# Gathering the experts of 32 more tokens, four experts of a token per gather, with dense products over 352 tokens

## The chip, the cores and the metric

The kernel runs on one core of one Trainium2 chip. The metric is device time in microseconds, from one launch, as the median of several runs. A separate profiled execution gives the trace; its own time stands beside its span below.

## The reference

One decoder layer over 512 tokens of width 1024: a combined input projection, differential attention and retention, an output projection, then PEER (product-key single-neuron experts), then a gated per-layer input and a last RMSNorm. The change touches PEER alone, which is:

```python
def peer(m, w_query, sub_keys, u, v):        # u, v: (16384, 1024) f32
    qry = (m @ w_query).reshape(B, S, PEER_HEADS, 2, PEER_KEY_DIM)
    scores = jnp.einsum('bshcd,hckd->bshck', qry, sub_keys)
    vals, idx = lax.top_k(scores, PEER_TOPK)            # 16 of 128 keys, twice
    ...
    top_s, top_pos = lax.top_k(cand, PEER_TOPK)         # 16 of 256 pairs
    expert = jnp.take_along_axis(cand_idx, top_pos, axis=-1)
    gates = jax.nn.softmax(top_s, axis=-1)
    ...
        act = jax.nn.gelu(jnp.einsum('cd,ced->ce', xt, u[e])) * g
        return jnp.einsum('ce,ced->cd', act, v[e])
```

Each token so has 8 heads x 16 = 128 experts out of 16384, each a row of `u` and a row of `v`. With `m` the normed input, the layer goes on as `h += peer(m)`, `h += sigmoid(rmsnorm(h) @ Wg + bg) * (p @ Wp)` and `out = rmsnorm(h)`.

## The kernel before

All is one function, `block_kernel`, with helpers inside. Four blocks of 128 tokens go through attention and the output projection; up to 368 us this has nothing to do with the change, but for `mtok` (line 920), the normed tokens of block 3.

PEER is computed in two ways. Blocks 0 to 2 (`NT = 3`, `ND = 384` tokens) go the dense way: for each of the 128 groups of 128 experts a product of U with all 384 tokens, Gelu, a multiplication by a map of gate weights (zero for experts that a token did not choose), and a product with V that is summed in PSUM. Block 3 goes the sparse way: each of its 128 experts per token is fetched by an indirect DMA of 128 rows, one row per token (`gather`, line 848), 4 KB each. A sparse step (`sparse_step`, line 853) is one VectorE instruction over 128x1024 elements: for `peer_u` a multiply and sum into a column of `act` (line 859), for `peer_v` a multiply and add into `yacc` (line 861). 256 of these steps are in the list `order` (lines 825 to 831), 128 of each kind.

Float32 products go over TensorE as three products of a high and a low part. For a U group (`products`, line 766, through `project` and `product3`, line 85) these are 24 matmuls with 128x128 of U as weights and 384 token columns moving; for a V group (line 782) 18 matmuls with 128 tokens of the activations as weights, 512 columns of V moving. `prepare` (line 736) makes the parts: ACT copies the high part `wh` (line 746), VectorE subtracts for the low part `wl` (line 762); for V groups VectorE also multiplies map and activation (`av`, line 752) and makes `al` (line 764), ACT makes `ah` (line 755). Weights are loaded by SP's queue four groups ahead (`RAW = 4`), their parts are made two ahead.

The first PEER stage (the loop at line 1190, 96 groups before) computes U groups only. Beside them `choose(b)` (line 1006) finds the 16 experts of each head, for block 3 first, and `weights_map(b, z)` (line 1111) builds the map, eight tokens in a pass: four VectorE instructions of 128x1024 (lines 1163 to 1166), 16 small matmuls (lines 1123, 1125), ACT copies to `gs` and `kept`. A map of 32 tokens is written to DRAM (`g_d`); activations of U groups past the first 24 are spilled to DRAM (`a_d`). What VectorE does between two groups is set by a small clock in the loop, which counts costs written in the code (`clock["pe"] += 4.1` for a group and so on). The number of groups in this stage comes out of that loop (`n_early`).

The second stage (the loop at line 1378) does the rest of the U groups and all V groups in the order of the list `seq`. Before it a budget is made: each load, write and gather of 512 KB counts `LOAD = 1.46`, `level` is the sum over the groups, and a sparse step is issued behind a group as long as

```python
            while done[0] < n_sp and (traffic + LOAD <= level * passed or n >= total - SPARSE_END):
                sparse_step()
                gather()
                traffic += LOAD
```

holds, so that the DMA traffic is spread evenly. Rows land in three buffers (`ROWS`), and in six more (`MORE`) from the time when the map's buffers are free until eight groups before `END = total - 64`; then the space goes to the closing part and three are left. Eight groups before the end the sparse sum is added to block 3 (`add_experts`, line 1258). Then follow the gate product, the sigmoid and the last norm (`turn`, `gate`, `close`).

Of the kernel before, what the change touches and what calls it, by code (L numbers as in the profile page):

```python
# [35 lines left out]
P = 128  # L36
S = 512
# [3 lines left out]
ND = NT * P  # L41
# [13 lines left out]
def block_kernel(ctx: ExitStack, tc, t):  # L55
# [89 lines left out]
    with pool("wa", 2, side="right") as wa, pool("sm", 2, side="right") as sm, \  # L145
# [553 lines left out]
        act = late.tile([P, P], F32, name="act")  # L699
        junk = late.tile([P, D], BF16, name="junk")  # L700
# [35 lines left out]
        def prepare(u, low):  # L736
            kind, i = u
            w = raw.pop(u)
            if kind == "g":
                for d in range(2):  # L740
                    c = slice(d * S, (d + 1) * S)
                    scaled_split(fin["gh"][i][d], fin["gl"][:, i, c], w[:, c], gains[:, G_PLE, i:i + 1])
                return
            wh = wt.tile([P, D], F32R, name="wh", tag="wh")
            wl = wt.tile([P, D], F32R, name="wl", tag="wl")
            nc.scalar.activation(wh, w, AF.Copy)  # L746
            parts[u] = wh, wl
            if kind == "v":
                gv, av = inputs.pop(u)
                if gv is not None:  # L750
                    av3 = av.rearrange("p (z t) -> p z t", t=RUN)
                    nc.vector.tensor_tensor(av3, gv, av3, op=OP.mult)  # L752
                ah = vp[0].tile([P, ND], F32R, name="ah", tag="ah", bufs=2)
                al = vp[0].tile([P, ND], F32R, name="al", tag="al", bufs=2)
                nc.scalar.activation(ah, av, AF.Copy)  # L755
                parts[u] += ah, al
            if low is nc.gpsimd:

                nc.scalar.activation(wl, w, AF.Copy, scale=-1.0)
                nc.gpsimd.dma_start(wl.bitcast(F32), w, accum_op=OP.add)  # L760
            else:
                low.tensor_tensor(wl, w, wh.bitcast(F32), op=OP.subtract)  # L762
            if kind == "v":
                nc.vector.tensor_tensor(al, av, ah.bitcast(F32), op=OP.subtract)  # L764
# [55 lines left out]
        vp, acc, count, done_u = [], [], [0], []  # L820
# [5 lines left out]
        for h in range(HEADS + 1):  # L826
            for k in range(TOPK):
                if h < HEADS:
                    order.append(("peer_u", h * TOPK + k))
                if h > 0:  # L830
                    order.append(("peer_v", (h - 1) * TOPK + k))
# [4 lines left out]
        def gather():  # L836

            while due:
                more = due.pop(0)
                if issued[0] >= n_sp or (more and not extra):  # L840
                    continue
                n = issued[0]
                issued[0] += 1
                table, r = order[n]
# [3 lines left out]
                nc.gpsimd.indirect_dma_start(out=rows[n], out_offset=None, in_=t[table],  # L848
                                             in_offset=bass.IndirectOffsetOnAxis(ap=e_sp[:, r:r + 1], axis=0))
# [3 lines left out]
        def sparse_step():  # L853
            n = done[0]
            done[0] += 1
            table, r = order[n]
            row = rows.pop(n)
            if table == "peer_u":
                nc.vector.tensor_tensor_reduce(junk, row, mtok, 1.0, 0.0, OP.mult, OP.add, act[:, r:r + 1])  # L859
            else:  # L860
                nc.vector.scalar_tensor_tensor(yacc, row, act[:, r:r + 1], yacc, op0=OP.mult, op1=OP.add)  # L861
            due.append(at_more.pop(n))
            if table == "peer_u" and r % TOPK == TOPK - 1:
                hs = slice(r + 1 - TOPK, r + 1)
                nc.scalar.activation(act[:, hs], act[:, hs], AF.Gelu)
                nc.vector.tensor_tensor(act[:, hs], act[:, hs], g_sp[:, hs], op=OP.mult)

        with pool("wp", 2, side="right") as wpp:
# [51 lines left out]
            nc.vector.tensor_tensor(mtok, mn[3], gffn, op=OP.mult)  # L920
    k_stack = ctx.enter_context(ExitStack())
    g_stack = ctx.enter_context(ExitStack())
    with pool("pk") as pk, pool("psG", 2, space=PSUM) as psG, pool("psT", space=PSUM) as psT:
# [74 lines left out]
        mh = pk.tile([P, ND], F16, name="mh")  # L998
        ml = pk.tile([P, ND], F16, name="ml")
        it = pk.tile([P, ND], BF16, name="it")  # L1000
        jt = pk.tile([P, ND], BF16, name="jt")
# [4 lines left out]
        def choose(b):  # L1006
# [77 lines left out]
            if b >= NT:  # L1084
# [4 lines left out]
                return  # L1089
            turned = []  # L1090
# [88 lines left out]
        def side():  # L1179
            yield from choose(3)  # L1180
            for b in range(NT):
                yield from choose(b)
                for z in range(P // RUN):
# [56 lines left out]
    def open_fin():  # L1240
# [10 lines left out]
        for name in ("gate_b", "final_gain"):  # L1251
            fin[name] = fp.tile([P, D], F32, name=name, bufs=1)
# [67 lines left out]
    with pool("acc", space=PSUM) as pa:  # L1320
        vp.append(mp)
        acc += [[pa.tile([P, S], F32, name=f"acc{b}{d}") for d in range(2)] for b in range(NT)]
# [30 lines left out]
        ends = [("hs", b) for b in (3, 0, 1, 2)] + [("final_gain", None), ("gate_b", None)]  # L1353
# [24 lines left out]
        for n, u in enumerate(seq):  # L1378
# [32 lines left out]
            if 0 <= n - end_at < len(ends):  # L1411
                name, b = ends[n - end_at]
                if b is None:
                    nc.sync.dma_start(fin[name], row_src(name))
                else:
                    nc.sync.dma_start(fin[name][:, b], sources[name][:, b])
# [96 lines left out]
```

## Time and profile before

| | us |
|---|---|
| median of 3 runs (lowest to highest) | 1546.71 (1545.36 to 1548.38) |
| the profiled execution: its time | 1544.91 |
| its span, first to last instruction | 1543.1 |
| TensorE busy | 1515.5 |
| VectorE busy | 1223.0 |
| ScalarE (ACT) busy | 676.4 |
| GpSimd (POOL) busy | 384.1 |
| DMA: bytes moved, mean over the span | 401.67 MB, 260 GB/s |
| granted TensorE clock, mean | 0.995 |

Busy time of TensorE is the union of its matmuls, whose ends are modelled: a matmul is drawn longer than the distance to the next. So the distance from start to start, or a piece of the chain divided by its matmuls, tells what one costs. The same holds in a small way for VectorE, where neighbours overlap by 0.08 us. The DMA share is the busy time of the 16 DMA engines over the stretch; packets overlap a little, so that it can read up to 1.03. A line number such as L85 can be that of a helper.

### The profile page before, as it was taken

What the parts mean: (1) busy time and instruction counts of PE and PEld (TensorE: products, weight loads), DVE (VectorE), ACT (ScalarE), POOL (GpSimd) and SP (SyncE); (2) the same over time, 40 slices, a digit from 0 to 9 for tenths busy, and PEclk for the clock granted to TensorE, in tenths of its full rate; (3) what the DMA queues carried; (4) which work ended last, traced back from release to release, by engine and by line L of the source; (5) the groups of instructions that cost most, each with busy time, mean ns of one, the idle gap of its engine ahead of it and who ended that gap; (6) DMA issues with size and microseconds to landing.
All of it is one profiled execution on the core that took longest, in us unless ns stands there. A gap on an engine that the chain in (4) does not pass through costs nothing.

```text
span 1543.1 us, 22928 instructions
## 1 busy us (share of the span) xinstructions
PE 1515.5 (98%) x8197; PEld 1342.0 (87%) x8197; DVE 1223.0 (79%) x2529; ACT 676.4 (44%) x1075; POOL 384.1 (25%) x321
## 2 busy tenths in 40 slices
PE   8999999999999999999999999999999999999996
PEld 6787887888999999999999989898988888888885
DVE  3767555779998999898985888988888885987755
ACT  4554645444634454453434333333333333453444
POOL 1300000110023203202224555554434311422000
PEclk9999999999999999999999999999999999999999
DMA  6412335773468979887999989999999988999601
GB/s 230 148 62 80 103 107 205 215 189 110 161 205 276 299 239 306 303 287 251 308 312 372 382 315 377 343 377 393 365 355 368 348 323 314 352 377 354 243 17 41
DMA packets 163378, 401.67 MB, mean 260 GB/s; under 512 B 14687, under 2 KB 77418, under 8 KB 163136
## 3 DMA queue, kind: packets, MB, share of 16 engines
q1 hardware_dynamic: 123248, 256.06, 46.7%
q0 software_dynamic: 40016, 144.15, 27.6%
q8 instruction: 64, 1.05, 0.3%
q14 instruction: 50, 0.41, 0.1%
HBM read 350.61 MB, written 42.21 MB: 255 GB/s over the span
## 4 chain that ended last, share of the span: by engine, by line
PE 88%; DVE 7%; DMA 3%; ACT 1%; issue 1%; SPq 0%; ACTq 0%; DVEq 0%
PE ps L85 44%; PE acc L782 31%; PE S L85 2%; PE S L322 2%; PE ps L518 1%; PE pg L1123 1%; PE pg L1125 1%; PE wo L85 1%; DVE wl L762 1%; PE sc L957 1%; DMA wraw<-in_w_val_dram 1%; DMA av<-a 1%; PE po L458 1%; PE po L639 1%; DMA wraw<-in_gate_w_dram 1%
## 5 line engine op out<-in xcount | busy, mean ns | idle before, releaser
L85 PE MATMUL ps<-xh,wh 128*128 128x384 f32 (+1 forms) x1312 | 464.0, 354 | 1.6 <-ACT av L810 0.8
L85 PE MATMUL ps<-xh,wl 128*128 128x384 f32 (+1 forms) x1312 | 457.3, 349 | 3.4 <-DVE wl L762 3.4
L85 PE MATMUL ps<-xl,wh 128*128 128x384 f32 (+1 forms) x1320 | 457.9, 347 | 0.0
L762 DVE TENSOR_TENSOR wl<-wraw,wh 128x1024 fp32r<-128x1024 f32 x260 | 317.4, 1221 | 77.5 <-ACT wh L746 76.8
L746 ACT ACTIVATE wh<-wraw 128x1024 fp32r<-128x1024 f32 x272 | 286.7, 1054 | 201.2 <-PE ps L85 94.7
L848 POOL DMA_INDIRECT row<-in_peer_u_dram,e_sp x128 | 174.0, 1359 | 360.6 <-DVE yacc L861 225.4
L848 POOL DMA_INDIRECT row<-in_peer_v_dram,e_sp x128 | 169.6, 1325 | 374.2 <-DVE act L859 277.3
L85 PEld LDWEIGHTS ps<-xh,wl 128*128 128x128 f32 x1312 | 247.4, 189 | 15.7 <-DVE wl L762 4.1
L85 PEld LDWEIGHTS ps<-xh,wh 128*128 128x128 f32 x1312 | 247.9, 189 | 13.9 <-ACT av L810 1.1
L85 PEld LDWEIGHTS ps<-xl,wh 128*128 128x128 f32 x1320 | 249.2, 189 | 10.2
L782 PE MATMUL acc<-wh,ah 128*128 128x512 f32 x768 | 237.1, 390 | 0.6 <-ACT ah L755 0.6
L782 PE MATMUL acc<-wl,ah 128*128 128x512 f32 x768 | 236.8, 390 | 0.0
L782 PE MATMUL acc<-wh,al 128*128 128x512 f32 x768 | 236.7, 390 | 0.0
L782 PEld LDWEIGHTS acc<-wl,ah 128*128 128x128 f32 x768 | 144.2, 188 | 30.1
L782 PEld LDWEIGHTS acc<-wh,al 128*128 128x128 f32 x768 | 144.2, 188 | 30.0 <-DVE al L764 0.2
L782 PEld LDWEIGHTS acc<-wh,ah 128*128 128x128 f32 x768 | 144.0, 188 | 30.1 <-ACT ah L755 1.0
L861 DVE SCALAR_TENSOR_TENSOR yacc<-row,act,yacc 128x1024 f32<-128x1024 f32 x128 | 163.9, 1280 | 2.0 <-DMA row<-in_peer_v_dram,e_sp 1.8
L859 DVE CUSTOM_DVE_ANT_0 junk<-row,mtok 128x1024 bf16<-128x1024 f32 x128 | 156.0, 1219 | 1.9 <-DMA row<-in_peer_u_dram,e_sp 1.6
L755 ACT ACTIVATE ah<-av 128x384 fp32r<-128x384 f32 x104 | 54.6, 525 | 228.5 <-PE acc L782 179.3
L764 DVE TENSOR_TENSOR al<-av,ah 128x384 fp32r<-128x384 f32 x104 | 57.8, 556 | 63.0 <-ACT ah L755 62.8
L1133 ACT ACTIVATE gs<-pg 128x832 f32<-128x832 f32 x48 | 41.6, 866 | 144.8 <-PE pg L1125 144.8
L752 DVE TENSOR_TENSOR av<-gv,av 128x384 f32<-128x384 f32 x104 | 57.5, 553 | 7.4 <-DMA av<-a 6.8
(288 smaller groups left out, 1686.4 us busy)
## 6 DMA issues: line engine op xcount, KB each, us to landing
wraw<-in_u_t_dram SPq DMA_DIRECT2D x128, 512.0 KB, 5.8
wraw<-in_peer_v_dram SPq DMA_DIRECT2D x128, 512.0 KB, 6.8
gv<-g_d SPq DMA_DIRECT2D x26, 768.0 KB, 8.4
a<-av SPq DMA_DIRECT2D x72, 192.0 KB, 4.2
g_d<-gs SPq DMA_DIRECT2D x24, 576.0 KB, 7.4
av<-a SPq DMA_DIRECT2D x72, 192.0 KB, 6.1
wraw<-in_w_in_t_dram SPq DMA_DIRECT2D x16, 512.0 KB, 3.3
wraw<-in_wq_t_dram SPq DMA_DIRECT2D x16, 512.0 KB, 4.1
```

Source lines behind the costliest of these rows:

```text
L85: nc.tensor.matmul(out, a, b, start=first and k == 0, stop=last and k == n - 1)
L322: nc.tensor.matmul(out, *((a, b) if q_first else (b, a)), start=n == 0, stop=n == 1)
L746: nc.scalar.activation(wh, w, AF.Copy)
L752: nc.vector.tensor_tensor(av3, gv, av3, op=OP.mult)
L755: nc.scalar.activation(ah, av, AF.Copy)
L762: low.tensor_tensor(wl, w, wh.bitcast(F32), op=OP.subtract)
L764: nc.vector.tensor_tensor(al, av, ah.bitcast(F32), op=OP.subtract)
L782: nc.tensor.matmul(acc[b][d], a[:, c], bb[:, d * S:(d + 1) * S], start=f, stop=l)
L848: nc.gpsimd.indirect_dma_start(out=rows[n], out_offset=None, in_=t[table], in_offset=bass.IndirectOffsetOnAxis(ap=e_sp[:, r:r + 1], axis=0))
L859: nc.vector.tensor_tensor_reduce(junk, row, mtok, 1.0, 0.0, OP.mult, OP.add, act[:, r:r + 1])
L861: nc.vector.scalar_tensor_tensor(yacc, row, act[:, r:r + 1], yacc, op0=OP.mult, op1=OP.add)
L1133: nc.scalar.activation(gs[0][:, :, t0:t0 + 8], pgi[:, KEEP:], AF.Copy, scale=2.0 ** -15)
```

## The change

32 of the 384 dense tokens, the last 32 of block 2, go the sparse way too. A gather has 128 rows, and for these tokens it takes four experts of each of the 32 (`QX = 4`): partitions 0 to 31 hold the first quarter of the expert list for the 32 tokens, 32 to 63 the second, and so on. So their 32 x 128 experts take 32 gathers of `u` and 32 of `v`. Their tokens are copied four times into `mtok_x`, their experts and gates into `e_x` and `g_x` by eight small DMAs in `choose(2)`. The four partial sums of a token in `yacc_x` are folded into the PSUM accumulators of block 2 by two float32 matmuls with a 0/1 matrix `fold`, eight groups before the end. U products and Gelu, `av`, `al`, `ah`, the map and its DRAM copies take 352 tokens; the left operands of the V products lie in three pairs of tiles of 384 columns, whose last 32 stay zero. The constants `gate_b` and `final_gain` are loaded into `mtok_x` and `mtok` eight groups before the end.

```diff
 NT = 3
-ND = NT * P
+NX = 32
+ND = NT * P - NX
+QX = P // NX
...
-                ah = vp[0].tile([P, ND], F32R, name="ah", tag="ah", bufs=2)
-                al = vp[0].tile([P, ND], F32R, name="al", tag="al", bufs=2)
-                nc.scalar.activation(ah, av, AF.Copy)
+                ah, al = pads[0]
+                pads.append(pads.pop(0))
+                nc.scalar.activation(ah[:, :ND], av, AF.Copy)
...
         order = []
-        for h in range(HEADS + 1):
-            for k in range(TOPK):
-                if h < HEADS:
-                    order.append(("peer_u", h * TOPK + k))
-                if h > 0:
-                    order.append(("peer_v", (h - 1) * TOPK + k))
+        for x, n in ((0, P // TOPK), (1, NX // TOPK)):
+            for h in range(n + 1):
+                for k in range(TOPK):
+                    if h < n:
+                        order.append(("peer_u", x, h * TOPK + k))
+                    if h > 0:
+                        order.append(("peer_v", x, (h - 1) * TOPK + k))
...
-                nc.vector.tensor_tensor_reduce(junk, row, mtok, 1.0, 0.0, OP.mult, OP.add, act[:, r:r + 1])
+                nc.vector.tensor_tensor_reduce(junk, row, (mtok, mtok_x)[x], 1.0, 0.0, OP.mult, OP.add, ac[:, r:r + 1])
             else:
-                nc.vector.scalar_tensor_tensor(yacc, row, act[:, r:r + 1], yacc, op0=OP.mult, op1=OP.add)
+                y = yacc_x[0] if x else yacc
+                nc.vector.scalar_tensor_tensor(y, row, ac[:, r:r + 1], y, op0=OP.mult, op1=OP.add)
...
             nc.vector.tensor_tensor(mtok, mn[3], gffn, op=OP.mult)
+            nc.vector.tensor_tensor(mn[2], mn[2], gffn, op=OP.mult)
+            for q in range(QX):
+                nc.gpsimd.dma_start(mtok_x[q * NX:(q + 1) * NX], mn[2][P - NX:])
...
+            if b == NT - 1:
+
+                ef = pk.tile([P, HEADS, TOPK], F32, name="ts", tag="ts")
+                ei = pk.tile([P, P], I32, name="pos", tag="pos")
+                nc.vector.scalar_tensor_tensor(ef, ij[:, 0], float(NKEY), ij[:, 1], op0=OP.mult, op1=OP.add)
+                nc.vector.tensor_copy(ei, ef.rearrange("p h k -> p (h k)"))
+                gx = ij[:, 2].rearrange("p h k -> p (h k)")
+                for q in range(QX):
+                    for x, y in ((e_x, ei), (g_x, gx)):
+                        nc.gpsimd.dma_start(x[q * NX:(q + 1) * NX], y[P - NX:, q * NX:(q + 1) * NX])
+                yield 0.5
...
-                for z in range(P // RUN):
+                for z in range((min(ND, b * P + P) - b * P) // RUN):
...
+        yacc_x.append(mp.tile([P, D], F32, name="yacc_x", bufs=1))
+        nc.gpsimd.memset(yacc_x[0], 0.0)
+        fold = mp.tile([P, P], F32, name="fold", bufs=1)
+        nc.gpsimd.memset(fold, 0.0)
+        for q in range(QX):
+            r = slice(q * NX, (q + 1) * NX)
+            nc.scalar.activation(fold[r, P - NX:], ident[r, r], AF.Copy)
+        for k in range(3):
+            pads.append([mp.tile([P, NT * P], F32R, name=f"a{z}{k}", bufs=1) for z in "hl"])
+            for x in pads[k]:
+                nc.scalar.activation(x[:, ND:], ident[:, :NX], AF.Copy, scale=0.0)
...
                 add_experts(3, [yacc[:, d * S:(d + 1) * S] for d in range(2)])
+                for d in range(2):
+                    nc.tensor.matmul(acc[NT - 1][d], fold, yacc_x[0][:, d * S:(d + 1) * S], start=False, stop=False)
+                for name in ("final_gain", "gate_b"):
+                    nc.sync.dma_start(fin[name], row_src(name))
```

The code of the loops' clocks and of the budget is unchanged, but what they count is not: the first stage now comes out at 88 groups instead of 96, and 61 instead of 65 sparse steps are done when it ends; `order` has 320 entries instead of 256, and the budget `level`, in units of its own, is 4.55 per group instead of 4.09.

The order of VectorE's instructions in the second stage shows it. First a place in its first half, before the change (`junk,act` and `act` are a `peer_u` step, `yacc` a `peer_v` step; `wl` marks a group):

```order
L752 TENSOR_TENSOR av<-gv,av 128x384
L762 TENSOR_TENSOR wl<-wraw,wh 128x1024
L764 TENSOR_TENSOR al<-av,ah 128x384
L859 ISA junk,act<-row,mtok 128x1024
L859 ISA act 128x1
L752 TENSOR_TENSOR av<-gv,av 128x384
L762 TENSOR_TENSOR wl<-wraw,wh 128x1024
L764 TENSOR_TENSOR al<-av,ah 128x384
L861 SCALAR_TENSOR_TENSOR yacc<-row,act,yacc 128x1024
L859 ISA junk,act<-row,mtok 128x1024
L859 ISA act 128x1
```

And about the same place after it:

```order
L769 TENSOR_TENSOR wl<-wraw,wh 128x1024
L771 TENSOR_TENSOR al_8431<-kept,ah_8430 128x352
L871 SCALAR_TENSOR_TENSOR yacc<-row,act,yacc 128x1024
L868 ISA junk,act<-row,mtok 128x1024
L868 ISA act 128x1
L769 TENSOR_TENSOR wl<-wraw,wh 128x1024
L771 TENSOR_TENSOR al_8435<-kept,ah_8434 128x352
L871 SCALAR_TENSOR_TENSOR yacc<-row,act,yacc 128x1024
L868 ISA junk,act<-row,mtok 128x1024
L868 ISA act 128x1
```

Where one or two steps stood behind a group, there are now two behind nearly every one. The second place is the last block of U groups, when three row buffers are left; on VectorE before:

```order
L762 TENSOR_TENSOR wl<-wraw,wh 128x1024
L859 ISA junk,act<-row,mtok 128x1024
L859 ISA act 128x1
L861 SCALAR_TENSOR_TENSOR yacc<-row,act,yacc 128x1024
L762 TENSOR_TENSOR wl<-wraw,wh 128x1024
L859 ISA junk,act<-row,mtok 128x1024
L859 ISA act 128x1
L762 TENSOR_TENSOR wl<-wraw,wh 128x1024
L861 SCALAR_TENSOR_TENSOR yacc<-row,act,yacc 128x1024
L762 TENSOR_TENSOR wl<-wraw,wh 128x1024
```

And after:

```order
L769 TENSOR_TENSOR wl<-wraw,wh 128x1024
L868 ISA junk,act_x<-row,mtok_x 128x1024
L868 ISA act_x 128x1
L769 TENSOR_TENSOR wl<-wraw,wh 128x1024
L871 SCALAR_TENSOR_TENSOR yacc_x<-row,act_x,yacc_x 128x1024
L868 ISA junk,act_x<-row,mtok_x 128x1024
L868 ISA act_x 128x1
L769 TENSOR_TENSOR wl<-wraw,wh 128x1024
L871 SCALAR_TENSOR_TENSOR yacc_x<-row,act_x,yacc_x 128x1024
L868 ISA junk,act_x<-row,mtok_x 128x1024
L868 ISA act_x 128x1
L769 TENSOR_TENSOR wl<-wraw,wh 128x1024
```

Here too the steps, now on `mtok_x` and `yacc_x`, come two to a group; over seven groups at this place there are 15 of them, where 12 stood.

## Rows read from the trace of the kernel before

**Rows 1.** The page's first part: busy us (share of the span) x instructions.

```profile
PE 1515.5 (98%) x8197; PEld 1342.0 (87%) x8197; DVE 1223.0 (79%) x2529; ACT 676.4 (44%) x1075; POOL 384.1 (25%) x321
```

**Rows 2.** Stages: window, length, busy us by engine, PEclk, DMA share, GB/s.

```profile
368.00:826.00 458.00, 451.85 (x3083) 443.14 (x3082) 409.23 (x913) 207.85 (x306) 93.73 (x73) 0.99 0.79 262
368.00:430.00 62.00, 56.67 (x316) 55.61 (x314) 61.17 (x272) 33.85 (x41) 3.06 (x3) 0.97 0.39 134
...
826.00:1443.00 617.00, 616.44 (x2899) 532.99 (x2899) 518.41 (x667) 234.83 (x326) 249.84 (x184) 1.00 0.96 357
1443.00:1484.00 41.00, 41.00 (x186) 33.99 (x185) 23.09 (x39) 16.28 (x24) 0.00 (x0) 1.00 0.33 113
1484.00:1543.00 59.00, 47.32 (x241) 39.78 (x239) 32.97 (x74) 28.61 (x53) 2.74 (x3) 0.94 0.10 36
```

**Rows 3.** Three stretches of the chain of waits: start us, us, what.

```profile
543.43 25.02 PE ps L85 x144
...
315.48 5.47 PE ps L85 x24
...
94.41 4.31 PE ps L518 x36
```

**Rows 4.** The chain of waits, a run of V products.

```profile
945.91 61.24 PE acc L782 x270
```

**Rows 5.** Timeline of TensorE: one map pass and the matmul after it (start, us).

```profile
803.55 0.24 PE L1123 MATMUL pg<-w 128*128 128x128 f16 x1
...
804.46 0.42 PE L85 MATMUL ps<-xh,wh 128*128 128x384 f32 x1
```

**Rows 6.** Groups by line, TensorE, 30 to 60 us: plain float32.

```profile
L339 PE MATMUL pb<-bucket,relw 33*128 33x512 f32 x2 | 1.1, 642 | 0.0
```

**Rows 7.** Timeline of VectorE, three row buffers: start, us, what [idle before].

```profile
1311.68 1.23 DVE L762 TENSOR_TENSOR wl<-wraw,wh 128x1024 fp32r<-128x1024 f32 x1 [1.59 <-ACT wh L746]
1312.82 1.22 DVE L859 CUSTOM_DVE_ANT_0 junk<-row,mtok 128x1024 bf16<-128x1024 f32 x1
...
1314.39 1.28 DVE L861 SCALAR_TENSOR_TENSOR yacc<-row,act,yacc 128x1024 f32<-128x1024 f32 x1 [0.34 <-DMA row<-in_peer_v_dram,e_sp]
1315.60 0.55 DVE L752 TENSOR_TENSOR av<-gv,av 128x384 f32<-128x384 f32 x1
...
1318.46 1.23 DVE L859 CUSTOM_DVE_ANT_0 junk<-row,mtok 128x1024 bf16<-128x1024 f32 x1 [0.71 <-DMA row<-in_peer_u_dram,e_sp]
...
1320.84 1.28 DVE L861 SCALAR_TENSOR_TENSOR yacc<-row,act,yacc 128x1024 f32<-128x1024 f32 x1 [1.14 <-DMA row<-in_peer_v_dram,e_sp]
```

**Rows 8.** Groups by line, VectorE, first stage: one instruction of a map pass.

```profile
L1163 DVE TENSOR_TENSOR Bl<-io,it 128x1024 f16<-128x1024 bf16 x33 | 22.6, 686 | 0.0
```

**Rows 9.** Waits of VectorE, first stage: us in total, times, longest.

```profile
DVE wl L762 <- ACT wh L746: 39.1, 33, 4.6
```

**Rows 10.** Instructions on the row buffers, 1302 to 1345 us; durations in ns.

```profile
L848 POOL DMA_INDIRECT row<-in_peer_v_dram,e_sp x8: 936/1074/3748, 1302.2 to 1341.3; - x8
...
L848 POOL DMA_INDIRECT row<-in_peer_u_dram,e_sp x6: 937/1012/3749, 1304.2 to 1333.5; - x6
...
DMA to landing us min/median/max: 4.8/7.8/10.6
```

**Rows 11.** DMA issues: x count, KB each, median us to landing.

```profile
wraw<-in_u_t_dram SPq DMA_DIRECT2D x128, 512.0 KB, 5.8
...
gv<-g_d SPq DMA_DIRECT2D x26, 768.0 KB, 8.4
...
av<-a SPq DMA_DIRECT2D x72, 192.0 KB, 6.1
```

**Rows 12.** Short stretches of the second stage, columns as in rows 2.

```profile
826.00:851.00 25.00, 25.00 (x135) 23.60 (x135) 19.20 (x24) 9.63 (x15) 14.06 (x10) 1.00 1.03 413
...
1006.00:1031.00 25.00, 25.00 (x135) 23.52 (x134) 20.54 (x27) 9.21 (x14) 14.00 (x11) 1.00 1.02 409
...
1241.00:1251.00 10.00, 10.00 (x57) 9.70 (x56) 9.35 (x14) 4.86 (x7) 2.02 (x2) 1.00 0.61 205
```

More of the change, by code (lines that the diff above doesn't have):

```diff
@@ L699, in block_kernel @@
         act = late.tile([P, P], F32, name="act")
+        mtok_x = late.tile([P, D], F32, name="mtok_x")
+        e_x = late.tile([P, NX], I32, name="e_x")
+        g_x = late.tile([P, NX], F32, name="g_x")
+        act_x = late.tile([P, NX], F32, name="act_x")
+        yacc_x = []
         junk = late.tile([P, D], BF16, name="junk")
@@ L763, in prepare @@
             if kind == "v":
-                nc.vector.tensor_tensor(al, av, ah.bitcast(F32), op=OP.subtract)
+                nc.vector.tensor_tensor(al[:, :ND], av, ah[:, :ND].bitcast(F32), op=OP.subtract)
         def products(u):
@@ L818, in spill @@
                 nc.sync.dma_start(*spills.pop(0))
-        vp, acc, count, done_u = [], [], [0], []
+        vp, acc, count, done_u, pads = [], [], [0], [], []
         writes, spills = [], []
@@ L843, in gather @@
                 issued[0] += 1
-                table, r = order[n]
+                table, x, r = order[n]
                 where, bufs = (extra["p"], MORE) if more else (late, ROWS)
@@ L848, in gather @@
                 nc.gpsimd.indirect_dma_start(out=rows[n], out_offset=None, in_=t[table],
-                                             in_offset=bass.IndirectOffsetOnAxis(ap=e_sp[:, r:r + 1], axis=0))
+                                             in_offset=bass.IndirectOffsetOnAxis(ap=(e_sp, e_x)[x][:, r:r + 1], axis=0))
         at_more, MORE = {}, 6
@@ L855, in sparse_step @@
             done[0] += 1
-            table, r = order[n]
+            table, x, r = order[n]
             row = rows.pop(n)
+            ac = (act, act_x)[x]
             if table == "peer_u":
-                nc.vector.tensor_tensor_reduce(junk, row, mtok, 1.0, 0.0, OP.mult, OP.add, act[:, r:r + 1])
+                nc.vector.tensor_tensor_reduce(junk, row, (mtok, mtok_x)[x], 1.0, 0.0, OP.mult, OP.add, ac[:, r:r + 1])
             else:
-                nc.vector.scalar_tensor_tensor(yacc, row, act[:, r:r + 1], yacc, op0=OP.mult, op1=OP.add)
+                y = yacc_x[0] if x else yacc
+                nc.vector.scalar_tensor_tensor(y, row, ac[:, r:r + 1], y, op0=OP.mult, op1=OP.add)
             due.append(at_more.pop(n))
@@ L864, in sparse_step @@
                 hs = slice(r + 1 - TOPK, r + 1)
-                nc.scalar.activation(act[:, hs], act[:, hs], AF.Gelu)
-                nc.vector.tensor_tensor(act[:, hs], act[:, hs], g_sp[:, hs], op=OP.mult)
+                nc.scalar.activation(ac[:, hs], ac[:, hs], AF.Gelu)
+                nc.vector.tensor_tensor(ac[:, hs], ac[:, hs], (g_sp, g_x)[x][:, hs], op=OP.mult)
         with pool("wp", 2, side="right") as wpp:
@@ L997, in block_kernel @@
         gsp = g_stack.enter_context(pool("gsp", side="right"))
[L998 to L1001, printed above, removed]
+        mh = pk.tile([P, NT * P], F16, name="mh")
+        ml = pk.tile([P, NT * P], F16, name="ml")
+        it = pk.tile([P, NT * P], BF16, name="it")
+        jt = pk.tile([P, NT * P], BF16, name="jt")
         later, soon = [], []
@@ L1250, in open_fin @@
         fin["gl"] = fp.tile([P, KC, D], F32R, name="gl", bufs=1)
-        for name in ("gate_b", "final_gain"):
-            fin[name] = fp.tile([P, D], F32, name=name, bufs=1)
+        fin["gate_b"], fin["final_gain"] = mtok_x, mtok
         fin["st"] = fp.tile([P, 8], F32, name="st", bufs=1)
@@ L1352, in block_kernel @@
         last_kept = max(n for n, u in enumerate(seq) if u[0] == "v" and u[1] < KEEP)
-        ends = [("hs", b) for b in (3, 0, 1, 2)] + [("final_gain", None), ("gate_b", None)]
+        ends = [("hs", b) for b in (3, 0, 1, 2)]
         ends += [("pl", b) for b in (3, 0, 1, 2)]
@@ L1412, in block_kernel @@
                 name, b = ends[n - end_at]
[L1413 to L1416, printed above, removed]
+                nc.sync.dma_start(fin[name][:, b], sources[name][:, b])
             if n == total - 8:
```

## The prediction, before the changed kernel was timed

> **What bounds the kernel now.** I read the page's busy line first [rows 1]: TensorE 98%, VectorE 79%, so the end is set where TensorE stops or slows. Then the stages [rows 2]. From 368 to 826 us lie the U products of the first 96 expert groups, with the choosing of experts and the weight map beside them: TensorE busy 451.9 of 458 us, VectorE 409.2. From 826 to 1443 us lie the other 32 U products and most V products, with most of the gathers: TensorE 616.4 of 617 us, VectorE 518.4, the DMA engines at a share of 0.96 and 357 GB/s. From 1443 to 1484 us only V products are left (DMA share 0.33), and after 1484 comes the closing part, which the change leaves as it is. So TensorE bounds everything from 368 to 1484 us, but a second limit stands close behind in each stage: VectorE in the first, the DMA engines in the second. The change takes work from TensorE and gives work to these two, which is the whole question.
>
> **What a U product gains.** In the chain of waits 144 matmuls of 384 columns take 25.02 us, 24 of 512 take 5.47 and 36 of 256 take 4.31 [rows 3]: 173.8, 227.9 and 119.7 ns each. The line through them has 0.42 ns per column, so 352 columns should take 160.2 ns, 13.5 less. The weight load ahead of each matmul has the same 128x128 form in all three, and the 256-column row shows that it lets matmuls through every 120 ns; it is no floor at 160. A U product (24 matmuls) goes from 4.17 to 3.84 us; 128 of them save 41.6 us. The V products save nothing: their left operand is padded with zeros to 384 columns, so the six matmuls per term stay and 18 take 61.24 x 18/270 = 4.08 us as before [rows 4]. Four of 48 map passes go; one takes TensorE from 803.55 to 804.46 us [rows 5], so 3.6 us. Added are two float32 matmuls of 512 columns for the fold; the nearest row, two of that width in 1.1 us [rows 6], prices them at 1.1 us. TensorE alone would thus gain 44 us.
>
> **First stage.** The built program now has 88 U products in it instead of 96 (the other eight move to the second stage), 44 map passes instead of 48, and 61 sparse steps instead of 65. TensorE: minus 8 x 4.17, minus 88 x 0.33, minus 4 x 0.91 = 66 us, leaving 392 of 458. VectorE loses eight splits at 1.14 us (start to start, [rows 7]), four sparse steps at 1.2, and four map passes of four instructions at 0.69 less the 0.08 by which neighbours overlap [rows 7, 8]: 9.1 + 4.8 + 9.8 = 24, leaving 385 of 392. Of its idle time 39 us are waits for ACT's copy `wh` [rows 9], which itself waits for a buffer that TensorE frees; when TensorE is faster this shrinks by itself. So the gain lies between 24 us (VectorE keeps its 49 us of idle time on top of 385) and 66 us (it loses none). In the first 62 us VectorE was busy 61.2 us and TensorE still 56.7 [rows 2], so a full VectorE costs TensorE little by little, not in large gaps. I take 58 us, near the upper end. The new operations here hide: the product for `mtok_x` (one more 128x1024 instruction, 1.2 us by [rows 7]) runs on VectorE while TensorE does the query products, and the eight small copies for `e_x` and `g_x` stand on POOL's queue ahead of gathers that wait for later VectorE steps anyway. If that cover were gone they would cost about a gather's issue each, 8 x 1.1 us [rows 10], once.
>
> **Second stage, DMA.** Now 357 GB/s over 617 us are 220 MB [rows 2]. Added are 64 new gathers and the four that slip from the first stage, 128 rows of 4 KB each: 68 x 0.524 = 35.7 MB; and eight more loads of U (512 KB, [rows 11]): 4.2 MB. Off come a twelfth of each `gv` (26 x 64 KB = 1.7 MB), the `av` loads (72 of 192 KB become 64 of 176 KB: 2.6 MB) [rows 11], and two constants that move behind it (1.0 MB): 255 MB. TensorE would need 617 + 8 x 3.84 - 28 x 0.33 = 638 us for this stretch, so 400 GB/s are wanted throughout. What the DMA engines give is bounded from below by 357, the mean of a stretch in which TensorE and not they set the pace, and from above by the stretches of 25 us at full share, 413 and 409 GB/s [rows 12]. Where the share fell to 0.61 the rate was 205 in the same stage [rows 12]: the mean is low because requests were missing, so the true value is nearer to the upper rows. I take 395: 645 us, 28 more than now. The Trainium skill, "DMA: Bandwidth & Descriptors", section "Where 436 GB/s comes from", says that between HBM and SBUF the HBM side binds at about 358 GB/s per core; by that this stretch would take 712 us in place of 645; the 25 us rows at 413 and 409 disagree with it.
>
> **Second stage, row buffers.** In the last 60 products only three row buffers are left. There the trace of before shows 14 gathers issued from 1302.2 to 1341.3 us, 3.0 us each (7.8 us to land at the median, 10.6 at most) [rows 10], and VectorE waiting 0.7 and 1.1 us for rows [rows 7]. The new order asks for 15 steps in seven products (some 28 us) at one place, where three buffers give them in 45. The parts are made two products ahead, which covers some 8 us, and part of the rest is inside the 28 us above; I add 8 us, between 0 and 16. VectorE itself gets 68 x 1.2 + 8 x 1.14, less 0.03 on each of some 200 `av` and `al` (0.55 us at 384 columns, 1.22 at 1024 [rows 7]): 85 us more, 603 of 645: busy, but not the limit. The stretch from 1443 to 1484 us stays, since eleven products still follow the last sparse step. The fold (1.1) and ten small ACT copies at the start of the stage (1, the first waits for a memset on POOL) add 2. POOL has 68 more gathers at some 1.1 us on 250 busy of 617 us [rows 2, 10]; on SP's queue the two constants stand eight products before the end, behind the last sparse step that reads the tiles they overwrite, and only the last V loads are queued behind them: nothing for both.
>
> **Sum:** -58 + 28 + 8 + 2 = -20 us. The profiled execution took 1544.9 us (span 1543.1); the median of the runs is 1546.7, 1.8 more. So 1527 us.
>
> **The rivals.**
> (a) The DMA engines follow all the way, at 400 GB/s or more, and TensorE stays the bound: -66 + 21 + 2 = -43, 1504 us, or 1511 with the 58 of the first stage. For it: the 25 us rows at 409 and more [rows 12]. Against it: these were short, with full buffers, and VectorE would be at 94 to 98% beside.
> (b) The ring of three row buffers is the bound, slower or no change. Some 64 steps are left for it. If a row takes 10.6 us to land, as the slowest did [rows 10], a buffer comes round every 11.8 us and the steps take 64 x 11.8/3 = 252 us against some 205 us of products: 47 instead of about 17 in my sum (its 8 and a third of the 28), so 1557. It decides from a landing time of about 8.5 us on. For it: VectorE waits for rows there already. Against it: in the same place TensorE lost nothing before.
> (c) Full share carries only 357/0.96 = 372 GB/s as a mean over this mix: 685 us, +68 with the ring inside it, so -58 + 68 + 2 = +12, 1559; with less gained in the first stage, 1575.
> (d) A ceiling near the mean of before, 357 GB/s: 714 us, +97 - 58 + 2 = +41, 1588. For it: no stretch of 600 us went faster. Against it: TensorE was busy 616 of the 617 us, so nothing asked for more, and 25 us at 413 GB/s are over it [rows 12]. This is what the rule of the Trainium skill named above would give.
> (e) The U products do not get faster and the new work is paid in full: the first stage gains 8 x 4.17 + 4 = 37, the second loses 33 + 8 + 2: 1553. The 256-column row speaks against it.
>
> **How the numbers follow.** My forecast gets 0.47, (a) 0.17, (b) 0.12, (c) 0.16, (d) 0.06, (e) 0.02. A difference under 0.2% (3 us) is about what a measurement of this kernel cannot tell from no change. Faster takes 0.43 of the forecast and (a): 0.60. Within 0.2% I count 0.04 of the forecast's slow edge and half of (b): 0.10. The rest, half of (b), (c), (d) and (e), is slower: 0.30. The range from 1508 to 1566 leaves out the better half of (a), the worse part of (c), and (d): two in ten. Most of the chance lies on the fast side; the forecast's own range is 1515 to 1543.
>
> **What the new profile would show.** U matmuls 160 ns apart in the chain, V matmuls 227. The first V product some 50 to 60 us earlier than now, VectorE over 95% busy before it. In the second stage a DMA share of 1.0 or more and 390 to 400 GB/s over more than 600 us, TensorE idle 15 to 40 us in it, its waits ended by VectorE's `wl`, and VectorE's by rows or `av` landing. If TensorE has no idle time there, (a) holds; if the share is full at 370, (c); if the share is below 0.95 while VectorE waits for rows in the last 200 us, (b). I would be wrong in the first stage if the first V product comes less than 45 us earlier.

## The result, and the profile of the changed kernel

The changed kernel takes 1530.13 us (median of 4 runs, 1527.62 to 1535.69), the kernel before beside it 1546.29 us (4 runs, 1545.36 to 1548.38): a ratio of 0.9899, 95% interval 0.9869 to 0.9928. That is faster by 1.0%, 3 us above the predicted 1527. The profiled execution took 1530.78 us, 14.1 less than that of before.

The busy lines of the page of the changed kernel:

```profile
PE 1482.4 (97%) x8137; PEld 1301.2 (85%) x8137; DVE 1274.0 (83%) x2610; ACT 670.8 (44%) x1083; POOL 491.9 (32%) x399
...
GB/s 228 145 69 69 118 100 197 212 176 129 168 176 285 307 263 301 325 296 264 326 359 409 409 409 409 409 408 409 406 408 407 397 388 376 300 392 391 279 1 56
```

Against [rows 1] TensorE has 33 us less, VectorE 51 more, POOL 108 more. New is the run of ten slices at 406 to 409 GB/s (a slice is 38 us).

The stages of the changed kernel (window, its length, busy us of PE, PEld, DVE, ACT, POOL, then the granted clock, DMA share, GB/s), to be held against [rows 2]:

```profile
373.00:775.00 402.00, 388.53 (x2826) 379.78 (x2825) 382.37 (x880) 191.49 (x293) 92.27 (x74) 0.99 0.80 266
373.00:435.00 62.00, 53.29 (x316) 51.55 (x314) 60.99 (x270) 33.35 (x41) 3.07 (x3) 0.97 0.40 133
775.00:1441.00 666.00, 655.79 (x3143) 563.53 (x3142) 603.18 (x790) 249.13 (x354) 357.18 (x256) 0.99 1.01 392
792.00:1294.00 502.00, 501.33 (x2427) 433.34 (x2427) 474.41 (x621) 182.56 (x254) 300.95 (x218) 1.00 1.02 404
1294.00:1319.00 25.00, 18.78 (x101) 18.33 (x101) 14.95 (x20) 6.70 (x10) 10.11 (x8) 0.86 0.91 323
1319.00:1441.00 122.00, 119.78 (x522) 96.55 (x521) 106.10 (x141) 53.09 (x76) 40.11 (x26) 1.00 0.97 358
1441.00:1472.50 31.50, 31.50 (x143) 25.44 (x142) 15.25 (x28) 12.38 (x19) 0.00 (x0) 1.00 0.21 78
1472.50:1529.00 56.50, 47.05 (x239) 39.39 (x237) 32.61 (x74) 28.43 (x53) 2.74 (x3) 0.94 0.10 38
```

The starts of the U and V products on TensorE cut the span into four parts. Second stage here means all from the first U product after the first stage to the last V product.

| | before | after | difference | predicted |
|---|---|---|---|---|
| start, up to the first U product | 368.0 | 373.0 | +5.0 | 0 |
| first stage (96, now 88 U products) | 458.3 | 402.4 | -55.9 | -58 |
| second stage | 657.9 | 696.9 | +39.0 | +38 |
| closing part | 58.9 | 56.7 | -2.2 | 0 |
| sum | 1543.1 | 1529.0 | -14.1 | -20 |

Two pieces of the chain of waits of the changed kernel (start us, us, what) give the price of the products, as [rows 3, 4] did before:

```profile
943.73 44.88 PE acc L789 x198
988.61 15.46 PE ps L87 x96
```

A U matmul of 352 columns takes 15.46/96 = 161.0 ns (173.8 before), so that a U product of 24 of them is 0.31 us shorter; a V matmul takes 226.7 ns (226.8 before).

In the long stretch from 792 to 1294 us TensorE is busy 501.3 of 502 us, while the DMA engines carry 404 GB/s at a share of 1.02. So TensorE is the bound there and the DMA engines follow. VectorE is nearly full beside it for a part of this stretch, and TensorE still loses nothing:

```profile
842.00:1042.00 200.00, 200.00 (x965) 172.54 (x963) 198.92 (x260) 73.81 (x106) 140.79 (x100) 1.00 1.03 409
```

The U and V products of the second stage alone now take 40 x 3.86 + 128 x 4.08 = 677 us; the distances between neighbouring products show 16.7 us of loss beside them, 8.7 of it in one block of U products near 1302 us. In windows of 4 us, same columns, that place reads:

```profile
1300.00:1304.00 4.00, 4.00 (x27) 4.00 (x26) 3.77 (x5) 1.06 (x1) 2.65 (x3) 1.00 0.66 235
1304.00:1308.00 4.00, 2.02 (x13) 1.73 (x11) 0.85 (x2) 0.00 (x0) 1.66 (x1) 1.00 1.04 382
1308.00:1312.00 4.00, 0.00 (x0) 0.00 (x0) 3.65 (x5) 0.66 (x2) 1.80 (x2) 0.79 0.89 309
1312.00:1316.00 4.00, 3.76 (x13) 3.76 (x14) 4.00 (x7) 1.45 (x3) 1.78 (x2) 0.50 0.84 265
1316.00:1320.00 4.00, 4.00 (x20) 3.72 (x19) 2.29 (x3) 1.60 (x3) 1.30 (x2) 0.86 1.02 349
```

TensorE stands still for 6 us, and when it goes on the granted clock is 0.50 (the level of 1.2 GHz): 13 matmuls in 4 us where 27 stood before. What it stood for is in the waits of the same place (engine and line, what it waited for: us in total, times, longest):

```profile
PE ps L87 <- ACT av L817: 6.2, 1, 6.2
...
ACT ah L762 <- DVE av L759: 10.8, 2, 8.2
...
DVE junk L868 <- DMA row<-in_peer_u_dram,e_x: 5.2, 3, 4.6
DVE yacc_x L871 <- DMA row<-in_peer_v_dram,e_x: 4.9, 2, 3.2
```

Read from below, three engines hand one wait on. VectorE stands at a sparse step whose row has not landed; behind it in VectorE's order wait the `av` and `wl` of the next products; ACT, in order too, waits for `av`, and behind that wait stands the Gelu `av` (L817) that empties the PSUM tile TensorE needs. It is the place where three row buffers are left. From 1290 to 1325 us the chain of waits is made of landing rows for the greater part:

```profile
1294.22 8.04 DMA row<-in_peer_u_dram,e_x
...
1302.44 7.06 DMA row<-in_peer_u_dram,e_x
...
1311.14 7.77 DMA row<-in_peer_v_dram,e_x
...
1322.56 6.74 DMA row<-in_peer_v_dram,e_x
```

At the start, too, there is a wait that the kernel before does not have. From TensorE's waits and the chain, 262 to 300 us, of the changed kernel:

```profile
PE sc L970 <- DMA sk<-in_sk_t_dram: 3.3, 1, 3.3
```

```profile
272.73 0.04 issue
272.76 8.24 DMA sk<-in_sk_t_dram
281.00 0.14 issue
```

The sub-keys `sk` land 8.24 us after their issue at 272.76; the four copies that fill `mtok_x` were issued on POOL's queue between 270.8 and 272.3 us, just ahead of them. In the kernel before, with the same two loads of query weights ahead of them on SP's queue, the first sub-keys landed in 4.3 to 5.0 us.

### The profile page after: what moved, and what is told of

Read it like the earlier page. It is cut to its first block, busy times and chain, and to the rows that moved or that the text cites. A ratio compares the mean times of both kernels' runs of the same rounds, so it can differ in the third digit from the quotient of the medians.

```text
span 1529.0 us, 22968 instructions
## 1 busy us (share of the span) xinstructions
PE 1482.4 (97%) x8137; PEld 1301.2 (85%) x8137; DVE 1274.0 (83%) x2610; ACT 670.8 (44%) x1083; POOL 491.9 (32%) x399
## 4 chain that ended last, share of the span: by engine, by line
PE 77%; DVE 11%; DMA 7%; issue 2%; ACT 2%; SPq 1%; POOL 0%; ACTq 0%; DVEq 0%; POOLq 0%
PE ps L87 32%; PE acc L789 32%; PE S L87 3%; DMA wraw<-in_u_t_dram 3%; DVE wl L769 3%; DMA row<-in_peer_v_dram,e_x 2%; PE S L324 2%; PE ps L520 2%; DMA row<-in_peer_u_dram,e_x 1%; PE wo L87 1%; DVE junk L868 1%; PE sc L970 1%; PE pg L1149 1%; PE pg L1147 1%; ACT wh L753 1%
## 5 line engine op out<-in xcount | busy, mean ns | idle before, releaser
L87 PE MATMUL ps<-xh,wh 128*128 128x352 f32 (+1 forms) x1312 | 453.3, 346 | 12.1 <-ACT av L817 11.1
L87 PE MATMUL ps<-xh,wl 128*128 128x352 f32 (+1 forms) x1312 | 445.7, 340 | 6.8 <-DVE wl L769 6.8
L87 PE MATMUL ps<-xl,wh 128*128 128x352 f32 (+1 forms) x1320 | 446.4, 338 | 0.0
L856 POOL DMA_INDIRECT row<-in_peer_u_dram,e_sp x128 | 184.8, 1444 | 289.8 <-DVE yacc L871 133.5
L87 PEld LDWEIGHTS ps<-xl,wh 128*128 128x128 f32 x1320 | 250.9, 190 | 10.3
L762 ACT ACTIVATE ah<-av 128x352 fp32r<-128x352 f32 x104 | 51.9, 499 | 205.6 <-DVE av L759 183.3
L1157 ACT ACTIVATE gs<-pg 128x832 f32<-128x832 f32 x44 | 38.0, 866 | 109.0 <-PE pg L1149 105.5
L856 POOL DMA_INDIRECT row<-in_peer_v_dram,e_x x32 | 47.2, 1474 | 76.8 <-DVE yacc_x L871 37.4
L856 POOL DMA_INDIRECT row<-in_peer_u_dram,e_x x32 | 42.2, 1320 | 66.8 <-DVE act_x L868 29.9
```

Of the source, the lines that this page charges most:

```text
L87: nc.tensor.matmul(out, a, b, start=first and k == 0, stop=last and k == n - 1)
L762: nc.scalar.activation(ah[:, :ND], av, AF.Copy)
L1157: nc.scalar.activation(gs[0][:, :, t0:t0 + 8], pgi[:, KEEP:], AF.Copy, scale=2.0 ** -15)
```

## The experiments

**The same kernel again**, beside the next three:

> The changed kernel once more, unaltered, so that the next kernels have it on the same chip. Both theories: 1527 to 1534 us.

1527.46 us (4 runs, 1524.08 to 1533.05), before 1543.77 us (7 runs), ratio 0.9895, interval 0.9864 to 0.9927. In its profile TensorE loses 17.3 us in the second stage, 10.9 in the block of U products, and waits for `sk` again. So the places of loss are the same; the sums of this and the next three are held against this one.

**Row buffers kept longer.** The nine row buffers shrink to three eight products before END, so moving END moves that. It also moves the loads of `hs` and `pl` for the closing part; in the changed kernel these were issued from 1227 to 1255 us, some 50 us before the stop.

```diff
-        W_EVERY, END = 2, total - 64
+        W_EVERY, END = 2, total - 46
```

> END moves from 64 to 46 groups before the end, so that nine row buffers instead of three serve the gathers until the last block of U groups is nearly reached. Theory one, the ring of three row buffers costs the 9 us that TensorE loses between 1294 and 1319 us: most of it goes, 6 to 12 us less than the unaltered kernel, about 1520 us. Theory two, the DMA engines are full there and rows are late for that: nothing is gained, 1528 to 1533 us, and TensorE loses the 9 us at the same block of U groups.

1519.96 us (4 runs, 1518.96 to 1525.49), ratio 0.9849, interval 0.9821 to 0.9876: 7.5 us under the kernel again, with intervals that overlap a little, so the trace has to bear it out. The losses of TensorE in the second stage fall from 17.3 to 10.3 us, those in the block of U products from 10.9 to 4.8. VectorE's waits from 1270 to 1440 us, first of the kernel again:

```profile
DVE junk L868 <- DMA row<-in_peer_u_dram,e_x: 10.5, 4, 5.5
DVE yacc_x L871 <- DMA row<-in_peer_v_dram,e_x: 9.1, 5, 3.4
```

and with the later END:

```profile
DVE wl L769 <- ACT wh L753: 13.3, 14, 2.0
DVE av L759 <- DMA av<-a: 5.8, 4, 2.6
DVE junk L868 <- DMA row<-in_peer_u_dram,e_x: 4.7, 1, 4.7
...
DVE yacc_x L871 <- DMA row<-in_peer_v_dram,e_x: 1.4, 2, 1.2
```

Waits for rows fall from 19.6 to 6.1 us; what VectorE waits for most now is ACT, whose copies `wh` wait mostly for TensorE. So the stop near 1302 us is due to the ring of three row buffers; about half of the loss in that block stays.

**The copies of `mtok_x` later.** The product is written into `mtok_x` itself, whose last 32 partitions are then already right, and the other three copies are issued behind the first loads of `sk`.

```diff
-            nc.vector.tensor_tensor(mn[2], mn[2], gffn, op=OP.mult)
-            for q in range(QX):
-                nc.gpsimd.dma_start(mtok_x[q * NX:(q + 1) * NX], mn[2][P - NX:])
+            nc.vector.tensor_tensor(mtok_x, mn[2], gffn, op=OP.mult)
...
+                if c == 8:
+                    for q in range(QX - 1):
+                        nc.gpsimd.dma_start(mtok_x[q * NX:(q + 1) * NX], mtok_x[P - NX:])
```

> The copies that fill mtok_x are issued half way through the query products instead of just before them. Theory one, they hold up the first load of the score keys, for which TensorE waits 3.3 us: the wait goes, the first U group starts 3 to 4 us earlier, the whole takes 1526 to 1528 us. Theory two, the late load is chance of the one profiled execution: no difference from the unaltered kernel, 1530 us.

1525.42 us (4 runs, 1522.82 to 1529.29), ratio 0.9883, interval 0.9861 to 0.9905. By the times alone it can't be told from the kernel again (0.9895). The trace can tell: the wait for `sk` is gone, the first U product starts at 368.2 us, as in the kernel before, and the chain there is TensorE's alone:

```profile
276.57 0.89 PE sc L968 x8
277.46 5.46 PE ps L87 x24
282.93 0.89 PE sc L968 x8
```

The copies cause the wait; it is worth some 3 us of the 5 at the start. In the five profiles for 32 tokens with the early copies the first U product starts between 370.4 and 373.0 us, in the three with the late ones between 367.4 and 368.5, so the rest varies from run to run.

**U products over 384 tokens, the rest of the change kept.** The `xh` and `xl` of the products are 384 wide, so that the U products lose their gain and the gathers stay.

```diff
-                n = ND if kind == "u" else S
+                n = NT * P if kind == "u" else S
```

> U products run over all 384 tokens again; everything else of the change stays (the 32 further columns are computed and not read). Theory one, the gain is the 32 columns, at 0.33 us a group: the first stage gets 20 to 28 us longer, less than 28.6 because VectorE held TensorE up before, the second 8 to 13 us: 1560 to 1570 us, slower than the kernel before the change. Theory two, VectorE sets the first stage already: the first stage gets less than 12 us longer, 1540 to 1552 us.

1555.6 us (one run), 12 slower than before: between the two ranges, 4 us from the first. The stages decide for theory one. The price in its chain:

```profile
946.84 16.66 PE ps L87 x96
```

173.5 ns a matmul. The first stage takes 421.5 us (402.4 in the changed kernel, 400.9 again), the second 705.1 (696.9 and 696.5). So the 32 columns are worth 28 us of the whole: 20 of the 27 that 88 products of 0.31 us would give TensorE in the first stage, where VectorE stands close behind, and 8.4 in the second.

**Without the added gathers.** The list of steps ends with block 3, so that the experts of the 32 tokens are left out.

```diff
-        for x, n in ((0, P // TOPK), (1, NX // TOPK)):
+        for x, n in ((0, P // TOPK),):
```

> The changed kernel without the 64 added gathers and their 64 sparse steps: the experts of the 32 tokens are missing from the output. Everything else (352 columns, copies, fold, padded tiles) is kept. Theory one: the added rows cost the second stage only what TensorE lost there, 16.7 us in the profile of the changed kernel (8.7 of it in the last block of U products); without them the losses fall under 6 us, the second stage takes 680 to 687 us instead of 697, the DMA engines run below 380 GB/s in it, the first stage stays within 4 us of 402, and the time is 1513 to 1522 us. Theory two: the rows cost nothing or the losses come from something else (VectorE's splits, ACT): losses stay above 12 us and the time is 1524 us or more. Theory three: DMA transfers also slow the loads that TensorE waits for everywhere, so that the first stage too gets shorter: time under 1508.

1516.33 us (one run). Its second stage takes 683.3 us, TensorE loses 5.9 in it, and the first stage stays at 399.2. Its windows from 771 to 1424 and from 790 to 1290 us:

```profile
771.00:1424.00 653.00, 650.00 (x3144) 564.09 (x3144) 531.83 (x692) 248.46 (x354) 241.59 (x192) 1.00 0.94 349
790.00:1290.00 500.00, 500.00 (x2435) 435.94 (x2434) 417.35 (x541) 182.05 (x252) 204.38 (x165) 1.00 0.95 352
```

So 64 gathers and their steps, 33.6 MB and 72 us of VectorE (1202.2 us busy in all against 1274.0), cost 13 us, 11 of them in stops of TensorE, and nothing in the long stretch: there TensorE is as full at 404 GB/s with them as at 352 without. Theory one holds.

**64 tokens instead of 32.** How far is the DMA limit?

```diff
-NX = 32
+NX = 64
```

> The same change for 64 tokens instead of 32: two experts of each token per gather, 64 more gathers, dense U products over 320 tokens. Theory one (the DMA engines give about 408 GB/s at full share and no more; at 32 tokens TensorE is the bound by a little): the second stage has some 34 MB more to move, 295 MB, 723 us at 408 GB/s and some 31 us of V products behind them, about 750 us instead of 697, with TensorE idle 50 us or more in it at a DMA share of 1.03; the first stage shortens by 25 to 40 us; the time is 1540 to 1565 us. Theory two (the DMA engines give more when more is asked, 430 GB/s or over, or their demand stays hidden): the second stage stays under 710 us and the time is 1495 to 1515.

1605.41 us (one run), slower than before by 60 and more than either theory said. The first stage shortens by 29 us, but the second takes 796.8 us with 108.6 us of loss. Its windows:

```profile
800.00:950.00 150.00, 138.66 (x674) 113.54 (x673) 147.36 (x193) 49.61 (x75) 111.54 (x80) 1.00 1.03 409
950.00:1240.00 290.00, 263.75 (x1276) 224.27 (x1276) 273.75 (x360) 89.22 (x130) 202.06 (x142) 0.96 1.03 407
1240.00:1420.00 180.00, 150.35 (x674) 123.22 (x673) 139.56 (x188) 52.69 (x78) 65.50 (x57) 0.92 0.91 334
```

Two things are in it. Up to 1240 us the DMA engines carry 407 to 409 GB/s, the rate of the changed kernel, and now TensorE loses 59 us. The DMA engines need not be the cause. VectorE's own work fills 421 of these 440 us, and it waits for rows in 14 of the rest. My estimate from these figures: with every row at hand, and the steps in the same order, the stretch would still take 421 us, so no more than 19 of the 59 us can be due to late rows, and VectorE has at least 40. A limit of the DMA engines is not shown by this run.

Behind 1240 us the rate falls to 334 GB/s, VectorE is busy 140 of 180 us, and TensorE still loses 50 us. The bytes were as expected (385 GB/s over 766 us are 295 MB); it was wrong to count them all at 408.

**64 tokens, END later**, to learn what the second part is:

```diff
-        W_EVERY, END = 2, total - 64
+        W_EVERY, END = 2, total - 46
```

> The change for 64 tokens, with END 46 instead of 64 products before the last. With 64 tokens and END 64 the second stage took 797 us: up to 1250 us TensorE waited at a DMA share of 1.02 to 1.03 and 404 to 409 GB/s; from 1250 to 1400 us it waited at 286 to 348 GB/s, while VectorE waited for rows. Theory one (the first loss is the DMA engines' ceiling, the second the ring of three row buffers): the loss up to the last block of U products stays, at 404 to 409 GB/s; the loss behind it shrinks, the second stage takes 755 to 780 us, the time is 1562 to 1588 us. Theory two (both are the DMA engines' ceiling, in the second part at a lower rate for the kinds of transfer there): the time stays within 8 us of 1605.

1587.58 us (one run), at the upper end of what theory one said; the second stage takes 779.3 us. Its windows of the same stretches:

```profile
800.00:950.00 150.00, 139.18 (x668) 113.36 (x668) 146.00 (x191) 49.49 (x75) 110.25 (x79) 0.99 1.03 409
950.00:1240.00 290.00, 263.92 (x1275) 223.59 (x1274) 274.73 (x361) 88.89 (x131) 202.54 (x141) 0.96 1.03 407
1240.00:1420.00 180.00, 165.36 (x768) 140.91 (x767) 159.22 (x220) 64.61 (x95) 83.04 (x63) 0.95 0.99 385
```

The loss up to 1240 us stays (61 us, 59 before), that behind it falls from 50 to 33, and there the rate rises from 334 to 385 GB/s. So the low rate in that part was for want of row buffers. The first loss stands, as both VectorE (again 421 of 440 us) and the rate do, and this edit touches neither.

**Both edits that helped, together** (the later END and the later copies, as above):

> The two edits tried alone before, together: END 46 instead of 64 products before the last, so that nine row buffers last longer, and the copies of the tokens for the added rows issued behind the first loads of the sub-keys. Theory: the gains add, 6 to 8 us from the first and 2 to 3 from the second: 1516 to 1520 us, and no wait of TensorE for the sub-keys. Rival: the gain at the start is given back in the first stage, whose first 62 us VectorE bounds: 1519 to 1523.

1515.89 us (5 runs, 1514.20 to 1517.22) beside 1544.89 for before (9 runs): ratio 0.9812, interval 0.9799 to 0.9826. It beats both kernels with one of the edits and is just below the lower end of what the theory said; nothing is given back in the first stage (399.7 us). The second takes 688.5 us with 9.2 us of loss.

**And the six buffers kept four products longer still:**

```diff
-            if not extra and n < END - 12 and not writes:
+            if not extra and n < END - 8 and not writes:
...
-            if n == END - 8:
+            if n == END - 4:
```

> The version with both edits, and the six more row buffers kept four products longer, to four products ahead of END. Theory one (what TensorE still loses near END, some 5 us in the profile with the later END alone, is the three-buffer ring): losses there fall under 3 us and the time is 1 to 3 us below that of the version with both edits. Theory two (what is left comes from the tiles of the closing part that are opened there, which now wait for the rows): losses there stay at 5 us or grow, and the time is the same or up to 3 us more.

1516.26 us (5 runs, 1514.10 to 1518.33), ratio 0.9814, interval 0.9798 to 0.9829: the same. The loss near END moves from 1294 to 1312 us and stays, 4.8 us against 4.6, the numbers of theory two. A stop is left there even without the added gathers (2.9 us at 1294 us in that run). VectorE's waits around it, 1285 to 1310 us, without the added gathers:

```profile
DVE yacc L871 <- DMA row<-in_peer_v_dram,e_sp: 4.3, 2, 3.8
DVE wl L769 <- ACT wh L753: 3.7, 3, 1.7
```

In that run END is still 64 products before the last. Its ring had shrunk between 1190 and 1222 us, and the loads of `hs` and `pl` for the closing part were issued by 1246 us, so neither begins at the stop. The chain there has the late row, asked for as soon as a step had freed a buffer, at 1290.74 us:

```profile
1290.74 7.78 DMA row<-in_peer_v_dram,e_sp
```

So a stop can come wherever three buffers are left, whatever rows are in them. In the two runs with both edits these loads begin close to the stop, and whether the waiting row is late there because its buffer was held or for those loads, these runs don't tell.

## Why the prediction was right, and where not

The time and the two large terms came out (-55.9 for -58, +39.0 for +38), the second of them for a reason that was partly wrong, so that it is partly luck how close the sum came.

- **What a U product gains**: 160.2 ns predicted from the line through three widths [rows 3], 161.0 measured, so 0.31 us a product for 0.33. V products unchanged, as said.
- **First stage**: right, nearer to the upper bound. VectorE is busy 382.4 of 402 us (385 was worked out, of 392). The first V product comes 50.5 us earlier, in the 50 to 60 that were named. What was in [rows 2] and could have been read further: in the first 62 us VectorE is full, and the first 13 products take 62.6 us now and 62.4 before, so that piece gains nothing. In the whole stage TensorE's waits grew from 6.1 to 13.4 us, those ended by VectorE's `wl` from 3.4 to 6.8. The run with 384 columns shows the same from the other side: 20 of 27 us.
- **Second stage, DMA**: this is the step that failed: "I take 395: 645 us, 28 more than now." The DMA engines gave 404 GB/s as a mean over 502 us and 406 to 409 in ten slices together, and TensorE did not wait for them there. The rows of 25 us at 409 and 413 [rows 12], held back as "short, with full buffers", were the right price for 400 us too. TensorE's own 21 us are then the whole term, as in rival (a). The other argument against (a), VectorE nearly full beside it, cost TensorE nothing either (198.9 of 200 us busy from 842 to 1042). Two smaller slips: the stretch moved 261 MB (392 GB/s over 666 us), 6 more than were counted, and the sum took 28 x 0.33 us off TensorE's need where all 32 U products of the stretch gain (1.3 us). The Trainium skill ("DMA: Bandwidth & Descriptors", section "Where 436 GB/s comes from") has about 358 GB/s per core as the bound between HBM and SBUF; 404 GB/s measured over 502 us contradict it for this mix of loads and gathers. Rival (d) falls with the same number. So does rival (c), 372 GB/s at full share.
- **Second stage, row buffers**: the mechanism was right and in its place (the 15 steps in seven products, three buffers), and 8 us was a little small: 8.7 in the block of U products and 3.2 behind it in the changed kernel, 10.9 in the block alone in the second profile. The later END takes out 7.0 of 17.3 us, the gathers left out 11. Part of the loss is one that the sum did not have: after the stop TensorE runs at 0.50 of its clock. Rival (b), 47 us, needed rows that land in 8.5 us or more throughout; in the chain above they took 6.7 to 8.0, and the three-buffer stretch lost a quarter of that.
- **Fold and starts**: the fold costs 1.3 + 0.44 us where it stands (1.1 predicted), the start of the second stage 2.2.
- **What was costed at nothing and was not**: the prediction looked at VectorE's product for `mtok_x` and at the eight small copies for `e_x` and `g_x`, and not at the four copies that fill `mtok_x`, transfers just ahead of the loads of `sk`, for which TensorE waits. They cost some 3 us, so the part up to 368 us is not untouched by the change. The same rule that was kept for gathers (what stands behind it, and who waits for that) would have found it.
- **Signs**: the first V product, the two prices and the full DMA share came as named, and VectorE's sum for the second stage too (603 us worked out, 603.2 measured). One sign did not: TensorE's long wait was ended not by VectorE's `wl` but by ACT's Gelu, a step further along the same chain.
- The closing part is 2.2 us shorter; no run was made for that, and it is left open.

The errors cancelled in part: 7 us too many for the DMA engines, 3 to 4 too few for the ring, 2 for the start of the second stage, 5 for the start of the kernel (3 of them the copies), and 2 us more lost in the first stage.

So where did the 44 us that the change takes from TensorE go? At the measured prices they are 64 in the first stage less 21 of products and 2 of the fold in the second: 41. In the profile 8 of the 64 went to waits in the first stage, where VectorE stands close behind; 16 in the second stage (39.0 less 21 of products and 2 of the fold) to stops, some 13 of them due to the added rows; 5 to the start; 2 came from the closing part: 41 - 8 - 16 - 5 + 2 = 14. The two edits that take 8 us from the stops and the copies' wait away give 1515.89.

## What to carry to other kernels

A limit that the profile shows at full share for short stretches is a measured rate; a mean below it, in a stretch that something else paces, is no ceiling. Price added transfers by the full stretches, and look for the cost where buffers get few: a stop there can cost more than its length. And for every copy that is added, small ones too, look at which loads are issued in the same microseconds, and who waits for those.

## What the runs showed of the hardware that was not expected

- One core held 406 to 409 GB/s for some 380 us (ten slices), half of it and more in gathers of 4 KB rows, with TensorE busy for the whole of it. With more to move (64 tokens) the rate stayed at 407 to 409 and TensorE lost time; as VectorE was busy 421 of 440 us there, whether the DMA engines could give more is open.
- A stop of TensorE can cost twice. In the windows above it stood for 6 us and then ran at a granted clock of 0.50 for a stretch of 4 us: of the 8.7 us lost in that block 2.3 belong to the products after the stop. After a stop of 2.7 us in the run without the added gathers the window kept a clock of 1.00, and the next products lost nothing; after one of the same length with both edits together it fell to 0.90, and 1.7 us more were lost. What makes the difference was not tried. The window from 1290 to 1305 us, without the added gathers:

```profile
1290.00:1305.00 15.00, 12.31 (x77) 12.02 (x76) 10.52 (x16) 5.12 (x8) 5.50 (x5) 1.00 0.93 351
```

and with both edits together:

```profile
1290.00:1305.00 15.00, 12.26 (x67) 11.97 (x67) 9.20 (x13) 4.27 (x6) 5.60 (x5) 0.90 1.00 369
```

- Behind four copies of 128 KB each a load issued half a microsecond later took 8.24 us to land and TensorE waited 3.3 us for it. Without them ahead there was no wait in two profiles and 0.6 us in the third; with both edits together these loads landed in 4.0 to 4.7 us.
